# A DeltaNet encoder layer on one core: the first 16 tokens' products widened to 128 rows, and the inner products of a scan step moved into the next step

## Chip, core and metric

The kernel runs on one core of a Trainium2 chip. The metric is the device time of one execution in microseconds (us). The engines are TensorE (PE, with its weight loads as PEld), VectorE (DVE), ScalarE (ACT), GpSimd (POOL) and SyncE (SP), which issues most transfers.

## What is computed

One layer of an encoder over 16 learned tokens and 1024 tokens of input, D_MODEL 1024, 8 heads of 128. The part that the change touches is the gated delta rule, run forward and backward over the tokens in chunks, and summed:

```python
def step(S, inp):
    qk_c, qd_c, kd_c, u_c, w_c, gl_c = inp
    v_new = u_c - jnp.einsum("bhcd,bhde->bhce", w_c, S)
    o_c = (jnp.einsum("bhcd,bhde->bhce", qd_c, S)
           + jnp.einsum("bhij,bhje->bhie", qk_c, v_new))
    S = S * gl_c[..., None, None] + jnp.einsum("bhcd,bhce->bhde", kd_c, v_new)
    return S, o_c
...
o_fwd = chunk_gated_delta_rule(qp, kp, vp, gp[:, :, 0], bp[:, :, 0])
o_bwd = flip(chunk_gated_delta_rule(flip(qp), flip(kp), flip(vp), flip(gp[:, :, 1]), flip(bp[:, :, 1])))
o = (o_fwd + o_bwd)[:, META_PAD:]
```

Around it stand the input projection (q, k, v, z and gates), a short convolution as a second branch, the merge of both, an output projection, and a feed-forward block.

## The kernel before

**First part: dense products with scans in between.** The input projection runs as "units" of 128 output columns. A unit is `dense_steps` (L328): for each piece of tokens (320 to 512 columns) 24 products in a high/low split (hh, hl, lh). Between these dense products stand the steps of four streams, one head at a time in each: `g_decay`, `g_norm` (L537: transposes and squares of k and q, products k k and k q), `g_inv` (L640: inverse of the triangular blocks, L727 to L768) and `g_scan` (L772: the scan). A generator `yield`s the planned time at which it may go on; `run_streams` resumes it once PE's planned clock `T["pe"]` has got there. `pe(ns)` advances that clock, and `on(engine, ns)` books an operation of another engine, never earlier than PE's planned clock:

```python
T[e] = max(T[e], ready, T["pe"]) + ns
return T[e] + TOPE
```

So the planned times alone decide how many dense products stand between two groups of a stream. The program's order on each engine is written out by this plan; no engine leaves it when it runs. A head starts its stages when the heads ahead of it have freed what they hold. When the units are used up, the streams go on without dense work.

**The first 16 tokens ("meta").** They are a chunk of their own, number 8 in the head's tiles. `g_norm` transposes their k (L98 from L562) and forms k k (L563); `g_inv` inverts a 16x16 block on POOL and loads it as `Pm` (L698); `g_scan` multiplies it with the scaled v (L803), scales the result on DVE (`w`, L806) and multiplies with `kn` (L808); the result is the first state S0 (L811).

**A step of the scan** (8 steps per head, both directions `d` in each, chunks c = i and 7-i):

- b1 = k S (L853), b2 = q S (L856), in one group; then on DVE r0 (L863);
- NP r0 (L869); then on ACT w (L876) and v2 (L881);
- kn w (L886), then the new S on DVE (L899);
- the inner products PQ v2 (L890), which later go into the output: `output` takes q S (L831 on ACT or L834 on DVE), and what is put into `pending` (L839 adds the inner product, L843 squares the sum on ACT) is done by `outputs()` in the following step, after r0.

b1 and b2 come from the three PSUM banks of `pss`. After the last step `norm` scales the head's output on DVE (L915 to L923), and it is transposed (L98) and stored (L940).

**Second part.** The list SECTION (L1623) orders what follows: four z units (`z4` to `z7`, `dense` at L134 to L136, 48 products each, whose low weights `wl` DVE makes at L179), and DVE's preparation of sums and low parts (b0 to b3, mA, mB; L179 and L1407), then pair products (`product`, L1441), which read these sums. Each engine's order is fixed here, too.

Of the kernel before, what the change touches and what calls it, by code (L numbers as in the profile page):

```python
# [8 lines left out]
F32 = mybir.dt.float32  # L9
# [7 lines left out]
P = 128  # L17
# [3 lines left out]
META = 16  # L21
# [27 lines left out]
def encoder_layer(ctx: ExitStack, tc: tile.TileContext, x, meta, norm1_w, w_in, w_ba,  # L49
                  dn_conv_w, A_log, dt_bias, dn_norm_w, sc_conv_w, w_bdn, w_bsc,  # L50
                  w_out, norm2_w, w_gu, w_down, final_w, out):
    nc = tc.nc
# [12 lines left out]
    def uid(s):  # L65
        cnt["n"] += 1
        return f"{s}_{cnt['n']}"
# [29 lines left out]
    def transpose(dst, src, n=P):  # L97
        nc.tensor.transpose(dst, src, ident[:n, :n])  # L98
# [159 lines left out]
    def pe(ns):  # L258
        T["pe"] += ns
        return T["pe"] + HOP  # L260
# [4 lines left out]
    def A(n):  # L265
        return on("act", 144 + 0.834 * n)
# [204 lines left out]
    def cs(c):  # L471
        return slice(META + c * P, META + (c + 1) * P)
# [64 lines left out]
    def g_norm(h, st_):  # L537
# [23 lines left out]
        pt = psd()  # L561
        transpose(pt[:META, :P], kT[:, 0:META])  # L562
        mm(pt[:META, P:P + META], kT[:, 0:META], kT[:, 0:META], start=True, stop=True)  # L563
        t = pe(120)
        nxt = tok(0)
        yield t
        nc.scalar.copy(kn[:META, 8], pt[:META, :P])
        A(P)
# [69 lines left out]
        enqueue("norm", norm_job(st_, ssk1, cc, ce, he, y, tmp, sk))  # L638

    def g_inv(h, st_):  # L640

        NP, Nm = st_["NP"], st_["Nm"]

        nd = dr.tile([4, NC, 2, 32, 32], F32, tag="nd", name=uid("nd"), bufs=2)
# [47 lines left out]
        for b in range(4):  # L694
            nc.sync.dma_start(NP[B(b), :, :, B(b)].rearrange("j c d i -> j (c d) i"), pd[b].rearrange("c d j i -> j (c d) i"))
        Pm = dn.tile([META, META], F32, tag="Pm", name=uid("Pm"), bufs=2)
        st_["Pm"] = Pm
        nc.sync.dma_start(Pm, pdm)  # L698

# [72 lines left out]
    def g_scan(h, st_):  # L772
# [12 lines left out]
        for grp in ((8, 0, 7), (1, 2, 3), (4, 5, 6)):  # L785
            pt = newbank()
            for i, c in enumerate(grp):
                if c == 8:
                    transpose(pt[:META, i], vT[:, 0:META])
                else:  # L790
                    transpose(pt[:, i], vT[:, cs(c)])
            yield pe(330)
            for i, c in enumerate(grp):
                p = META if c == 8 else P
                nc.scalar.activation(vS[:p, c], pt[:p, i], AF.Copy, scale=sk[:p, c:c + 1])
                A(P)
# [5 lines left out]
        bank = newbank()  # L802
        mm(bank[:META, 0], Pm, vS[:META, 8], start=True, stop=True)  # L803
        yield pe(215)
        w = dn.tile([P, P], F32, tag="w0", name=uid("w"))
        nc.vector.tensor_scalar(out=w[:META], in0=bank[:META, 0], scalar1=ce[:META, 8, 0:1], scalar2=None, op0=ALU.mult)  # L806
        yield V(P, 1)
        mm(bank[:, 1], kn[:META, 8], w[:META], start=True, stop=True)  # L808
        yield pe(215)
# [4 lines left out]
        seen = set()  # L814
        pending = []

# [5 lines left out]
        def output(b2, c, d, sums):  # L822
# [3 lines left out]
            if not sums:  # L826
                nc.scalar.copy(oacc[c], b2[:, 2 + d])
                A(P)
                return
# [17 lines left out]
        for i in range(NC):  # L847
# [4 lines left out]
            for d in act_:  # L852
                mm(b1[:, d], kT[:, cs(cd[d])], S[d], start=True, stop=True)  # L853
            t = pe(215 * len(act_))
            for d in act_:
                mm(b2[:, d], qT[:, cs(cd[d])], S[d], start=True, stop=True)  # L856
# [26 lines left out]
            if i < NC - 1:  # L883
# [3 lines left out]
                t = pe(430)  # L887
            yield tv
            for d in range(2):
                mm(b2[:, 2 + d], PQ[:, cd[d], d], v2[d], start=True, stop=True)  # L890
            t2 = pe(430)
            if i < NC - 1:
                yield t
                for d in range(2):
# [7 lines left out]
                    S[d] = Sn  # L902
            else:
                freed += 1
                yield t2
# [1238 lines left out]
```

## Time and profile before

| | |
|---|---|
| median of 3 runs | 1980.38 us (1978.99 to 1980.45) |
| the profiled execution | 1978.97 us |
| its span, first to last instruction | 1977.2 us |
| TensorE clock granted | 0.999 |
| last scan's first transposes of v (L98) | at 873.1 us |
| z units on PE | 932.4 to 976.0 us |

A row of the timeline reads: start, length, engine, line, operation, out<-in, shapes, and in brackets idle time of the engine before it and what ended it. For matmuls, "16*128 16x128" is the stationary tile (rows*columns) and the moving one (rows x columns); "x4" counts instructions, and a product of 32-bit floats is two. The length of a product reaches over the start of the next one, since products are pipelined. A row of a stretch of time reads: from:to, length, then for PE, PEld, DVE, ACT and POOL the busy time (and instructions), then PE's granted clock, the share of the DMA engines and GB/s. L12 is line 12 of the kernel before.

### The profile page before, as it was taken

To read this page: it belongs to the slowest core of one execution; us is meant where nothing else is said; L and a number is where in the kernel's file an instruction comes from. 1 tells how busy PE (TensorE), PEld (TensorE's weight loads), DVE (VectorE), ACT (ScalarE), POOL (GpSimd) and SP (SyncE) were. 2 spreads that over 40 slices of the span, in tenths; PEclk is the share of its full clock that TensorE was granted. 3 is DMA by queue.
4 is the path that set the end of the run, shared out by engine and by line. 5 is a ranking of instruction groups with operands and counts; after the bars stand their busy time and mean duration, and the time that the engine had idled before them with its cause. 6 is when DMAs were issued, how large, how long until landed. Compare 5 with 4: busy or idle time off the path is not lost.

```text
span 1977.2 us, 31834 instructions
## 1 busy us (share of the span) xinstructions
PE 1961.2 (99%) x11992; PEld 1715.3 (87%) x11992; DVE 1395.8 (71%) x3017; ACT 838.5 (42%) x1968; POOL 106.6 (5%) x407
## 2 busy tenths in 40 slices
PE   9999999999999999999999999999999999999998
PEld 8999999999999999888888888888888888888887
DVE  7888688888888888844954544469676766746575
ACT  6472354636464646344444221225333333334344
POOL 2011101010101010100000000000000000000000
PEclk9999999999999999999999999999999999999999
DMA  4122122222222212222236752123366654477654
GB/s 145 59 88 81 55 87 60 76 60 76 60 76 60 76 60 76 70 87 90 102 128 229 252 167 97 65 86 111 124 220 243 253 183 165 170 278 243 193 176 165
DMA packets 124703, 251.52 MB, mean 127 GB/s; under 512 B 44988, under 2 KB 46453, under 8 KB 122117
## 3 DMA queue, kind: packets, MB, share of 16 engines
q1 hardware_dynamic: 123957, 248.44, 37.7%
q8 instruction: 94, 1.54, 0.3%
q10 hardware_dynamic: 592, 1.05, 0.1%
q14 instruction: 60, 0.49, 0.1%
HBM read 181.20 MB, written 68.25 MB: 126 GB/s over the span
## 4 chain that ended last, share of the span: by engine, by line
PE 92%; DVE 3%; DMA 2%; ACT 1%; issue 1%; SPq 0%; POOL 0%; DVEq 0%; POOLq 0%; ACTq 0%
PE pm L328 30%; PE pd L1441 14%; PE pe L1441 7%; PE pm L1441 5%; PE pe L136 2%; PE pe L135 2%; PE pe L134 2%; PE pd L869 1%; PE pd L890 1%; PE pd L853 1%; PE pe L2051 1%; PE pe L2052 1%; PE pe L2050 1%; PE pd L856 1%; PE pe L590 1%; PE pd L886 1%
## 5 line engine op out<-in xcount | busy, mean ns | idle before, releaser
L328 PE MATMUL pm<-hTh,wh 128*128 128x320 f32 (+4 forms) x1248 | 428.3, 348 | 0.3 <-ACT hTh L1091 0.2
L328 PE MATMUL pm<-al,wh 128*128 128x320 f32 (+4 forms) x1248 | 427.4, 348 | 0.0
L328 PE MATMUL pm<-hTh,wl 128*128 128x320 f32 (+4 forms) x1248 | 425.8, 346 | 0.1
L328 PEld LDWEIGHTS pm<-hTh,wh 128*128 128x128 f32 x1248 | 233.8, 188 | 12.8 <-issue 2.1
L328 PEld LDWEIGHTS pm<-hTh,wl 128*128 128x128 f32 x1248 | 233.9, 188 | 10.6 <-issue 0.4
L328 PEld LDWEIGHTS pm<-al,wh 128*128 128x128 f32 x1248 | 233.9, 188 | 9.7
L102 DVE TENSOR_TENSOR al<-raw,ring_h 128x1024 fp32r<-128x1024 f32 x73 | 88.6, 1222 | 64.7 <-ACT ring_h L101 63.9
L101 ACT CAST ring_h<-raw 128x1024 fp32r<-128x1024 f32 x73 | 76.6, 1053 | 106.2 <-PE pe L2052 35.0
L350 DVE SCALAR_TENSOR_TENSOR kq<-ra,wc,kq 128x520 f32<-128x520 f32 x128 | 96.5, 754 | 4.7 <-ACT kq L380 3.4
L977 DVE TENSOR_TENSOR wl<-raw,wh 128x512 fp32r<-128x512 f32 x112 | 75.8, 687 | 31.4 <-ACT wh L980 30.9
L876 ACT ACTIVATE w<-pd,small 128x128 f32<-128x128 f32 x128 | 39.8, 363 | 125.2 <-PE pd L869 124.6
L483 DVE TENSOR_TENSOR tm<-fP,fN 128x135 f32<-128x135 f32 (+23 forms) x248 | 71.6, 289 | 5.4 <-POOL mP L682 1.0
L487 DVE TENSOR_TENSOR fP<-fP,tm 128x135 f32<-128x135 f32 (+23 forms) x248 | 71.4, 288 | 5.1
L980 ACT CAST wh<-raw 128x512 fp32r<-128x512 f32 x112 | 66.3, 621 | 3.7 <-issue 3.6
L101 ACT CAST wh<-raw 128x1024 fp32r<-128x1024 f32 x37 | 38.8, 1048 | 46.6 <-PE pm L135 14.8
L1989 ACT ACTIVATE b<-b 128x512 f32<-128x512 f32 x20 | 12.6, 631 | 104.5 <-DVE b L1407 104.5
L843 ACT ACTIVATE jk<-NP 128x128 f32<-128x128 f32 x64 | 19.9, 311 | 76.5 <-DVE NP L839 75.4
L1441 PE MATMUL pd<-b_hl,wh 128*128 128x512 f32 x168 | 51.9, 390 | 0.0
L899 DVE SCALAR_TENSOR_TENSOR S<-S,eGl,pd 128x128 f32<-128x128 f32 x104 | 31.5, 340 | 28.0 <-PE pd L886 27.9
L863 DVE SCALAR_TENSOR_TENSOR r<-pd,negEG,vS 128x128 f32<-128x128 f32 x120 | 36.7, 344 | 20.4 <-PE pd L853 20.2
L1407 DVE TENSOR_TENSOR b<-pd,b 128x512 f32<-128x512 f32 x21 | 14.5, 689 | 51.8 <-PE pd L1441 51.8
L102 DVE TENSOR_TENSOR wl<-raw,wh 128x1024 fp32r<-128x1024 f32 x37 | 45.1, 1218 | 7.4 <-ACT wh L101 7.3
(629 smaller groups left out, 4783.0 us busy)
## 6 DMA issues: line engine op xcount, KB each, us to landing
raw<-in_w_in_dram SPq DMA_DIRECT2D x72, 512.0 KB
raw<-in_w_gate_up_dram SPq DMA_DIRECT2D x44, 512.0 KB
sums<-in_w_down_dram SPq DMA_DIRECT2D x22, 512.0 KB
t_d<-sums SPq DMA_DIRECT2D x11, 1024.0 KB
raw<-s_d SPq DMA_DIRECT2D x44, 256.0 KB
raw<-t_d SPq DMA_DIRECT2D x44, 256.0 KB
act_d<-b SPq DMA_DIRECT2D x43, 256.0 KB
raw<-act_d SPq DMA_DIRECT2D x33, 256.0 KB
```

What stands on the lines that cost most here:

```text
L101: nc.scalar.copy(hi, src)
L102: nc.vector.tensor_tensor(out=lo, in0=src, in1=hi.bitcast(F32), op=ALU.subtract)
L134: mm(po[:m, :n], wh[:, k, :m], xhk[:, t0:t0 + n], start=(k == 0), stop=False)
L135: mm(po[:m, :n], wh[:, k, :m], xlk[:, t0:t0 + n], start=False, stop=False)
L328: mm(po[:, :n], ww[:, k], f(k)[:, t0:t0 + n], start=i == 0, stop=i == 3 * KT - 1)
L350: nc.vector.scalar_tensor_tensor(out=acc, in0=raw[:, h0 + t:h0 + t + hn], scalar=wc[:, t, col:col + 1], in1=acc, op0=ALU.mult, op1=ALU.add)
L483: nc.vector.tensor_tensor(out=tv, in0=fP[:, 0:r, j:j + 1].broadcast_to([P, r, n]), in1=fN[:, j:j + 1, j + 1:32].broadcast_to([P, r, n]), o ...
L487: nc.vector.tensor_tensor(out=fP[:, 0:r, j + 1:32], in0=fP[:, 0:r, j + 1:32], in1=tv, op=ALU.subtract)
L876: nc.scalar.activation(w[d], b2[:, 2 + d], AF.Copy, scale=ce[:, c, d:d + 1])
L977: nc.vector.tensor_tensor(out=u[1][1][:, k], in0=u[2][:, k], in1=u[1][0][:, k].bitcast(F32), op=ALU.subtract)
L980: nc.scalar.copy(u[1][0][:, k], u[2][:, k])
L1441: mm(po, x[:, k], at(y, k), start=i == 0 and not add_to, stop=i == 11, skip_group_check=add_to)
```

## The change

It has two parts. The products of the first 16 tokens are taken over 128 rows and columns: k and v are transposed for tokens 0 to 127, k k is formed for 128, and the three tiles around the inverse (`Pm` for even and odd heads, and `w`) are full 128x128 tiles, filled with zeros once, of which only the 16 rows are written. And the inner products of a step (but the last) are no longer issued after kn w; they go into a list `late` that the following step issues between b1 and b2. The copy of the inner product in steps without a q S goes into `pending`.

```diff
-        transpose(pt[:META, :P], kT[:, 0:META])
-        mm(pt[:META, P:P + META], kT[:, 0:META], kT[:, 0:META], start=True, stop=True)
+        transpose(pt[:, :P], kT[:, 0:P])
+        mm(pt[:, P:2 * P], kT[:, 0:P], kT[:, 0:P], start=True, stop=True)
...
-        nc.scalar.copy(kn[:META, 8], pt[:META, :P])
+        nc.scalar.copy(kn[:, 8], pt[:, :P])
...
-        Pm = dn.tile([META, META], F32, tag="Pm", name=uid("Pm"), bufs=2)
-        st_["Pm"] = Pm
-        nc.sync.dma_start(Pm, pdm)
+        if not wide:
+            wide.extend(dn.tile([P, P], F32, tag=f"wide{i}", name=uid("wide")) for i in range(3))
+            for t in wide:
+                nc.gpsimd.memset(t, 0.0)
+        Pm = st_["Pm"] = wide[h % 2]
+        nc.sync.dma_start(Pm[:META, :META], pdm)
...
-                if c == 8:
-                    transpose(pt[:META, i], vT[:, 0:META])
-                else:
-                    transpose(pt[:, i], vT[:, cs(c)])
+                transpose(pt[:, i], vT[:, 0:P] if c == 8 else vT[:, cs(c)])
...
-        mm(bank[:META, 0], Pm, vS[:META, 8], start=True, stop=True)
+        mm(bank[:, 0], Pm, vS[:, 8], start=True, stop=True)
         yield pe(215)
-        w = dn.tile([P, P], F32, tag="w0", name=uid("w"))
+        w = wide[2]
...
-        mm(bank[:, 1], kn[:META, 8], w[:META], start=True, stop=True)
+        mm(bank[:, 1], kn[:, 8], w, start=True, stop=True)
...
             if not sums:
-                nc.scalar.copy(oacc[c], b2[:, 2 + d])
-                A(P)
+                def copy():
+                    nc.scalar.copy(oacc[c], b2[:, 2 + d])
+                    A(P)
+                pending.append(copy)
                 return
...
             t = pe(215 * len(act_))
+            while late:
+                late.pop(0)()
             for d in act_:
                 mm(b2[:, d], qT[:, cs(cd[d])], S[d], start=True, stop=True)
...
-            yield tv
-            for d in range(2):
-                mm(b2[:, 2 + d], PQ[:, cd[d], d], v2[d], start=True, stop=True)
-            t2 = pe(430)
+            def inner(b2=b2, cd=cd, v2=v2):
+                for d in range(2):
+                    mm(b2[:, 2 + d], PQ[:, cd[d], d], v2[d], start=True, stop=True)
+                return pe(430)
             if i < NC - 1:
+                late.append(inner)
                 yield t
...
             else:
+                yield tv
+                t2 = inner()
                 freed += 1
                 yield t2
```

Line numbers of the changed kernel stand a little higher: its L801, L806, L858, L871, L888, L892 and L928 are L803, L808, L856, L869, L886, L890 and L923 of before, and from the end of `g_scan` on all are 5 higher.

PE's order in the first head's scan, before: kn w, one dense product, the inner products, and dense products again.

```order
L886 MATMUL pd_2679<-w_2693,kn_1259 128x128
L886 MATMUL pd_2679<-w_2695,kn_1259 128x128
L328 MATMUL pm_2712<-hTh,wl_2457 128x322
L890 MATMUL pd_2680<-v_347_2697,PQ_1268 128x128
L890 MATMUL pd_2680<-v_348_2699,PQ_1268 128x128
L328 MATMUL pm_2712<-hTh,wh_2456 128x322
```

In the changed kernel, at the start of the following step:

```order
L853 MATMUL pd_2738<-S_2726,kq_308 128x128
L853 MATMUL pd_2738<-S_2728,kq_308 128x128
L892 MATMUL pd_2684<-v_348_2701,PQ_1268 128x128
L892 MATMUL pd_2684<-v_349_2703,PQ_1268 128x128
L858 MATMUL pd_2739<-S_2726,kq_308 128x128
L858 MATMUL pd_2739<-S_2728,kq_308 128x128
```

The inner products now stand between k S and q S, ahead of everything that waits for r0.

PE's order in the last head's scan, before, from the first products of a step to NP r0:

```order
L853 MATMUL pd_11990<-S_11979,kq_9467 128x128
L853 MATMUL pd_11990<-S_11981,kq_9467 128x128
L856 MATMUL pd_11991<-S_11979,kq_9467 128x128
L856 MATMUL pd_11991<-S_11981,kq_9467 128x128
L328 MATMUL pm_12010<-hTh,wh_11826 128x512
L328 MATMUL pm_12010<-al_124,wh_11826 128x512
L328 MATMUL pm_12010<-hTh,wl_11827 128x512
L328 MATMUL pm_12010<-hTh,wh_11826 128x512
L869 MATMUL pd_11991<-r_2047_11996,NP_10427 128x128
L869 MATMUL pd_11991<-r_2048_11998,NP_10427 128x128
```

And in the changed kernel, from a step's first products to kn w:

```order
L853 MATMUL pd_11936<-S_11930,kq_9924 128x128
L853 MATMUL pd_11936<-S_11932,kq_9924 128x128
L892 MATMUL pd_11905<-v_1999_11924,PQ_10037 128x128
L892 MATMUL pd_11905<-v_2000_11926,PQ_10037 128x128
L858 MATMUL pd_11937<-S_11930,kq_9924 128x128
L858 MATMUL pd_11937<-S_11932,kq_9924 128x128
L871 MATMUL pd_11937<-r_2005_11944,NP_10697 128x128
L871 MATMUL pd_11937<-r_2006_11946,NP_10697 128x128
L136 MATMUL pm_12177<-hTh,wl_12144 128x512
L134 MATMUL pm_12177<-hTh,wh_12143 128x512
L135 MATMUL pm_12177<-al_126,wh_12143 128x512
L888 MATMUL pd_11936<-w_11952,kn_10451 128x128
```

The units of the first part are used up by now; what stands between the last scan's groups are products of z4 and z5 (pm_12177 is the second half of z4), three at a time. After the last inner product (L890, now L892) and ahead of the first pair product stood 36 products of L328 and 192 of the z units; now there are 121 of the z units: the rest of z5 (25 products), z6 and z7.

DVE's order at the end of the last scan, before; NP is the head's output, wl_12158 the low weights of z5, b_2067 the first of the sums:

```order
L923 TENSOR_SCALAR NP_10427<-NP_10427,small_10129 128x128 x7
L465 SCALAR_TENSOR_TENSOR rb_12067<-rb_12067,pm_12010 128x512
L923 TENSOR_SCALAR NP_10427<-NP_10427,small_10129 128x128
L179 TENSOR_TENSOR wl_12158<-raw_12139,wh_12157 128x1024
L465 SCALAR_TENSOR_TENSOR rb_12119<-rb_12119,pm_12069 128x512
L179 TENSOR_TENSOR b_2067_12135<-hTh 128x2048
L179 TENSOR_TENSOR b_2068_12136<-al_124 128x2048
```

In the changed kernel:

```order
L499 SCALAR_TENSOR_TENSOR small_10449<-small_10449 128x9
L928 TENSOR_SCALAR NP_10697<-NP_10697,small_10449 128x128 x8
L179 TENSOR_TENSOR b_2054_12125<-hTh 128x2048
L179 TENSOR_TENSOR b_2055_12126<-al_124 128x2048
L1510 SCALAR_TENSOR_TENSOR s_2070_12203<-s_2070_12203,pe_12150 128x512
L1412 TENSOR_TENSOR b_2054_12125<-b_2054_12125,b_2055_12126 128x2048
```

The low weights of z5 and the gate operations (L465) stand ahead of the last scan now; the first of the sums still comes right after the head's last scaling, and the low weights of z6 seven operations further on, as before.

More of the change, by code (lines that the diff above doesn't have):

```diff
@@ L638, in g_norm @@
         enqueue("norm", norm_job(st_, ssk1, cc, ce, he, y, tmp, sk))
+    wide = []
     def g_inv(h, st_):
@@ L787, in g_scan @@
             for i, c in enumerate(grp):
-                if c == 8:
-                    transpose(pt[:META, i], vT[:, 0:META])
-                else:
-                    transpose(pt[:, i], vT[:, cs(c)])
+                transpose(pt[:, i], vT[:, 0:P] if c == 8 else vT[:, cs(c)])
             yield pe(330)
             for i, c in enumerate(grp):
-                p = META if c == 8 else P
-                nc.scalar.activation(vS[:p, c], pt[:p, i], AF.Copy, scale=sk[:p, c:c + 1])
+                nc.scalar.activation(vS[:, c], pt[:, i], AF.Copy, scale=sk[:, c:c + 1])
                 A(P)
@@ L814, in g_scan @@
         seen = set()
-        pending = []
+        pending, late = [], []
         def outputs():
```

## Prediction

> **What bounds the kernel now.** I read the page first, for the engine that is full.
>
> ```profile
> span 1977.2 us, 31834 instructions
> PE 1961.2 (99%) x11992; PEld 1715.3 (87%) x11992; DVE 1395.8 (71%) x3017; ACT 838.5 (42%) x1968; POOL 106.6 (5%) x407
> ```
>
> TensorE (PE) has something in flight 99% of the span, so two things change the time: products that cost PE more or less, and places where PE's fixed order makes it wait. A busy PE is not proof of full speed, because the ends of products are modelled; so I price products by the distance from one start to the next, in PE's own timeline. For the one place where another engine follows closely behind PE, I then read the end of the last scan: PE's timeline, VectorE's (DVE's), and the busy time in two stretches.
>
> ```profile
> 922.89 0.61 PE L890 MATMUL pd<-v,PQ 128*128 128x128 f32 x4
> ...
> 975.97 0.39 PE L1441 MATMUL pd<-hTh,wh 128*128 128x512 f32 x1
> ...
> 981.41 0.61 PE L1441 MATMUL pd<-b,mB 128*128 128x512 f32 x2
> ```
> ```profile
> 923.54 0.61 DVE L834 SCALAR_TENSOR_TENSOR NP<-pd,eG,NP 128x128 f32<-128x128 f32 x2 [1.17 <-PE pd L890]
> ...
> 929.21 0.68 DVE L465 SCALAR_TENSOR_TENSOR rb<-rb,pm 128x512 f32<-128x512 f32 x1
> 929.81 0.28 DVE L923 TENSOR_SCALAR NP<-NP,small 128x128 f32<-128x128 f32 x1
> ...
> 939.64 2.29 DVE L179 TENSOR_TENSOR b<-hTh 128x2048 f32<-128x2048 f32 x1 [4.31 <-DMA z_d<-rb]
> ...
> 951.04 1.22 DVE L179 TENSOR_TENSOR wl<-raw,wh 128x1024 fp32r<-128x1024 f32 x1
> ...
> 977.55 2.35 DVE L179 TENSOR_TENSOR mB<-raw,mB 128x1024 fp32r<-128x1024 f32 x2
> ```
> ```profile
> 932.43:975.97 43.54, 43.54 (x193) 36.04 (x192) 37.94 (x31) 15.86 (x20) 0.00 (x0) 1.00 0.33 115
> 939.64:979.90 40.26, 40.26 (x180) 33.32 (x179) 40.05 (x32) 16.69 (x19) 0.00 (x0) 1.00 0.23 83
> ```
>
> The last inner product of the last scan starts at 922.89. DVE then finishes the head: 923.54 to 929.81+0.28 = 930.09, with one gate operation (L465, 0.68 long) in between. From 939.64 DVE prepares the sums for the pair products of L1441, without a gap (columns of the stretches: length, busy PE, weight loads, DVE: 40.05 of 40.26). PE meanwhile runs 192 products of the z units, 43.54/192 = 0.227 each, and reaches the first pair product at 975.97 and, at 981.41, the first that reads those sums (mB, whose first half is done at about 977.55+1.2 = 978.8). So DVE is ahead by 2.7 us only. That distance is the tightest thing I found, and the change moves it.
>
> **Part 1: products over 128 rows.** The two products of a head's first 16 tokens:
>
> ```profile
> 214.40 0.34 PE L328 MATMUL pm<-al,wh 128*128 128x384 f32 x1
> 214.67 0.39 PE L803 MATMUL pd<-vS,Pm 16*16 16x128 f32 x2
> ...
> 215.27 0.34 PE L328 MATMUL pm<-hTh,wh 128*128 128x384 f32 x1
> 215.44 0.34 PE L328 MATMUL pm<-al,wh 128*128 128x384 f32 x1
> ...
> 215.97 0.34 PE L328 MATMUL pm<-al,wh 128*128 128x384 f32 x1
> 216.23 0.48 PE L808 MATMUL pd<-w,kn 16*128 16x128 f32 x2
> ...
> 216.93 0.34 PE L328 MATMUL pm<-hTh,wh 128*128 128x384 f32 x1
> ```
>
> From 214.40 to 215.27 PE did two dense products and L803; a dense product of 384 columns takes 215.44-215.27 = 0.17, two of them 0.35, so L803 costs 0.87-0.35 = 0.52. L808 costs 0.96-0.35 = 0.61. What a product of full size costs is seen in the scan steps:
>
> ```profile
> 420.55 0.60 PE L886 MATMUL pd<-w,kn 128*128 128x128 f32 x4
> 420.91 0.40 PE L328 MATMUL pm<-hTh,wh 128*128 128x336 f32 x1
> 421.14 0.61 PE L890 MATMUL pd<-v,PQ 128*128 128x128 f32 x4
> ...
> 423.46 0.61 PE L853 MATMUL pd<-S,kq 128*128 128x128 f32 x4
> 423.90 0.61 PE L856 MATMUL pd<-S,kq 128*128 128x128 f32 x4
> 424.27 0.40 PE L328 MATMUL pm<-al,wh 128*128 128x336 f32 x1
> 424.51 0.31 PE L328 MATMUL pm<-hTh,wl 128*128 128x336 f32 x1
> 424.66 0.32 PE L328 MATMUL pm<-hTh,wh 128*128 128x336 f32 x1
> ```
>
> Eight instructions (four products) and one dense product take 424.51-423.46 = 1.05; less the dense one (424.66-424.51 = 0.15 to 0.16) that is 0.89, or 0.22 a product. So L803 gives back 0.30 and L808 0.39. The head's opening group becomes dearer in one place:
>
> ```profile
> 99.26 0.27 PE L98 MATMUL pe<-ident,kq 128*16 128x128 f32 x1
> 99.46 0.21 PE L563 MATMUL pe<-kq 128*16 128x16 f32 x2
> 99.61 0.66 PE L98 MATMUL pe<-ident,kq 128*128 128x128 f32 x4
> ...
> 100.28 0.33 PE L328 MATMUL pm<-hTh,wh 128*128 128x384 f32 x1
> ```
>
> It takes 1.02 with one dense product, 0.85 without. With full sizes it is one transposition (0.11, half a product), one product (0.22) and four transpositions (0.44): 0.77, so 0.07 is saved although L563 has eight times the columns. The wider transposition of vT I set at nothing. Per head 0.76, for eight heads 6.0 us; I keep 5 to 7.
>
> The weight loads speak on the other side:
>
> ```profile
> L563 PEld LDWEIGHTS pe<-kq x16: 92/94/97, 99.5 to 765.1; 128*16 128x16 f32 x16
> L590 PEld LDWEIGHTS pe<-kq x128: 186/188/191, 114.0 to 795.1; 128*128 128x128 f32 x128
> ```
>
> A load of 16 columns takes 94 ns, one of 128 columns 188. The scan products have loads of 128 columns too and still follow each other every 0.11, so loads lie beside products and I add nothing. The Trainium skill ("TensorE: Matmul & The Clock Gate", section LDWEIGHTS) says that a load's time goes by its columns, columns/1.2 ns, whatever the rows; by its figures six wider loads a head would, if uncovered, take back an estimated 8 x 6 x 0.093 = 4.5 us of the gain.
>
> The memsets of the three tiles run once, on POOL (5% busy), and only the first head's Pm transfer stands behind them in SP's queue, long before L803 needs it: nothing, or a microsecond of PE if that cover were gone. The copies on ACT go over more partitions with the same 128 columns: nothing.
>
> **Part 2: the inner products moved.** On PE alone this is worth nothing. L886 by itself costs 0.36 and makes the next dense product 421.14-420.91 = 0.23 instead of 0.16 long: 0.44 in all. L853 and L856 merged cost 0.89, twice that. A group fewer saves no time. What changes is when the planner lets the rest follow. A VectorE operation is booked no earlier than PE's planned clock, and the inner products now advance that clock by 430 ns between a step's first products and its r0. Each of seven steps gets longer in the plan, in each of eight heads, so the same dense products are used up by earlier scans. The order shows the end of it: in the last scan no L328 is left, z products stand between its groups, and after its last inner product stand 121 z products where before there were 36 L328 and 192 z products. So 36+71 = 107 dense products, 107 x 0.227 = 24.3 us of PE, have moved ahead of that inner product.
>
> Now the order on DVE decides. The first preparation operation (b<-hTh) still stands behind the last scaling of the last head. It no longer has the transfer of L465 ahead (the 4.31 us wait at 939.64), because those operations stand earlier now. So, counted from the start of the last inner product:
>
> - DVE finishes the head: 930.09-922.89-0.6 = 6.6.
> - From b<-hTh to the end of the low weights of z6: 951.04+1.22-939.64 = 12.6. PE cannot start z6 before. It has 25 z products (5.7), eight transpositions (0.9) and the inner products (0.4) until then: 7.0 of 19.2, so it stands still for 12.2.
> - Then z6, z7 (96 x 0.227 = 21.8) and the first two pair products (981.41-975.97 = 5.4).
>
> The first product on mB thus starts 6.6+12.6+21.8+5.4 = 46.4 after the last inner product, against 981.41-922.89 = 58.5 before: 12.1 less, where PE's work became 24.3 less.
>
> The last scan itself must go through with little dense work beside it. A step of before:
>
> ```profile
> 907.64 0.61 PE L853 MATMUL pd<-S,kq 128*128 128x128 f32 x4
> ...
> 913.09 0.61 PE L853 MATMUL pd<-S,kq 128*128 128x128 f32 x4
> ```
> ```profile
> 908.29 0.61 DVE L863 SCALAR_TENSOR_TENSOR r<-pd,negEG,vS 128x128 f32<-128x128 f32 x2 [0.76 <-PE pd L853]
> ```
> ```profile
> 909.13 0.31 ACT L843 ACTIVATE jk<-NP 128x128 f32<-128x128 f32 x1 [3.29 <-DVE NP L839]
> ...
> 910.09 0.63 ACT L876 ACTIVATE w<-pd,small 128x128 f32<-128x128 f32 x2
> ```
>
> r0 starts 0.65 after its products and takes 0.61: 1.26, and PE now has 3 x 0.44 = 1.33 of work before it needs it. That fits, and the two other hops of a step look alike. In the last four steps the two squares (jk) hold ACT for some 0.9 us from 1.5 us after the step's start, and w is wanted at about 2.0: w comes some 0.3 late. That makes 4 x 0.3 = 1.2, and I add 0.6 for the short inverse ahead of the scan: 1.8, with 0 (all covered) and 7 (every hop 0.3 late) as bounds.
>
> **The sum.** The last inner product: +24.3 of moved work, -6.0 saved, +1.8 waits = +20.1. From there to the first product on mB: -12.1. Net +8.0, and behind it PE has no idle time that could take it up. The profiled execution took 1978.97 us (span 1977.2 and 1.8 around it), 1.4 below the median of the runs, 1980.38. 1978.97+8.0 = 1987.0; on the median 1988.4. With 5 to 7 saved and 0 to 7 of waits: +5.2 to +14.2.
>
> **The rivals.** *Only the products count.* If PE's queue never waited, the change would be -6.0: 1974.4. It decides where z6's weights are ready before PE has worked off what stands ahead of z6. For it: PE was 99% busy and the saving is seen in every head. Against it: z6 needs weights that DVE makes 19.2 us after the last inner product, and PE has 7.0 of work. 7%.
>
> *A group fewer is worth something.* If the 0.08 by which a dense product behind a group is longer were the price of a switch, 56 groups fewer would save 4.5 more: 1988.4-4.5 = 1983.9. The merged pair at 0.89 speaks against it. 5%. The Trainium skill ("TensorEngine Tiling (Array Packing)", section Key Properties) puts the switch elsewhere: changing the tiling mode drains TensorE. With the 128 cycles that "TensorE: Matmul & The Clock Gate" (step 4, drain) gives for a drain, two switches at each of L803 and L808 are an estimated 1.7 us over eight heads, under the 5.5 of the rows.
>
> *The last scan crawls.* If a step there cannot go under the 913.09-907.64 = 5.45 of before (against 3.6 of PE's work, 3.9 with my waits), seven steps cost 11 more: 1999. For it: ACT and DVE hold other work; against it: the hops above. 10%.
>
> *They cancel*, within 4 us: 3%.
>
> **How the numbers follow.** Forecast 75% at 1988.4. About 0.2%, 4 us, is what a measurement of this kernel can tell from no change. Faster by more: 7%. Within: the second rival and the cancelling, 8%. Slower by more: 85%. The forecast's own range is 1985.6 to 1994.6; down to 1983 it takes in the second rival, and up to 1996 the lower part of the crawling scan.
>
> **What would show it.** Right: L801 and L806 at about 0.22 each; no L328 after the last vT; PE idle for some 12 us before z6's first product, released by DVE's wl; the first product on mB about 46 us behind the last inner one. Wrong: PE without idle time there (then -6), or idle inside each step of the last scan (then more than +14).

## The result, and the profile after

The changed kernel takes 1989.68 us in the median of 6 runs (1988.32 to 1990.71), beside 1979.57 for before (6 runs, 1978.99 to 1980.45). The ratio is 1.0051, with a 95% interval of 1.0040 to 1.0062: slower by 10.1 us. The prediction said 1988.4, which is 8.0 more than its median of before. The profiled execution took 1989.04, 10.07 more than that of before.

The page gives no hint by itself. TensorE (PE) is as full as it was, and its busy time has hardly moved (1961.2 us in before):

```profile
PE 1961.0 (99%) x11992; PEld 1718.6 (86%) x11992; DVE 1403.6 (71%) x3017; ACT 838.5 (42%) x1968; POOL 110.9 (6%) x410
```

First the products of the first 16 tokens, in PE's timeline:

```profile
214.59 0.34 PE L328 MATMUL pm<-al,wh 128*128 128x384 f32 x1
214.77 0.38 PE L801 MATMUL pd<-vS,wide 128*128 128x128 f32 x2
214.91 0.42 PE L328 MATMUL pm<-hTh,wl 128*128 128x384 f32 x1
215.16 0.34 PE L328 MATMUL pm<-hTh,wh 128*128 128x384 f32 x1
```

From 214.59 to 215.16 PE did two dense products (0.35) and L801: 0.22 for L801, where L803 had cost 0.52. Then the end of the last scan, PE and VectorE (DVE):

```profile
941.26 0.49 PE L892 MATMUL pd<-v,PQ 128*128 128x128 f32 x2
...
958.72 0.80 PE L134 MATMUL pm<-hTh,wh 128*128 128x512 f32 x1 [9.43 <-ACT wh L1497]
...
960.68 0.80 PE L136 MATMUL pm<-hTh,wl 128*128 128x512 f32 x1 [0.74 <-DVE wl L179]
...
963.83 0.63 PE L134 MATMUL pm<-hTh,wh 128*128 128x512 f32 x1
964.26 0.63 PE L135 MATMUL pm<-al,wh 128*128 128x512 f32 x1
...
989.49 2.88 PE L1446 MATMUL pd<-b,mB 128*128 128x512 f32 x12
```
```profile
946.32 1.66 DVE L928 TENSOR_SCALAR NP<-NP,small 128x128 f32<-128x128 f32 x8
...
959.41 1.22 DVE L179 TENSOR_TENSOR wl<-raw,wh 128x1024 fp32r<-128x1024 f32 x1
...
985.93 2.35 DVE L179 TENSOR_TENSOR mB<-raw,mB 128x1024 fp32r<-128x1024 f32 x2
```

The last inner product starts at 941.26 (before: 922.89), so 18.4 later. From there to the first product on mB PE takes 48.2 (before: 58.5), of which it stands still for 9.43 ahead of z6 and for 0.74 ahead of z6's third product. The first product on mB starts at 989.49 instead of 981.41: 8.1 later. DVE works without a gap from the last scaling to mB.

One thing is new: behind the idle time the products of z6 follow each other every 0.43 (963.83 to 964.26), nearly twice the 0.23 that they take from 965 on. The table of stretches gives the granted clock (the column with 1.00, 0.50, 1.00). It falls in the middle of the idle time and comes back at 964.76:

```profile
948.35:954.52 6.17, 0.94 (x5) 0.42 (x3) 6.17 (x4) 1.08 (x2) 0.00 (x0) 1.00 0.72 255
954.52:964.76 10.24, 5.30 (x12) 3.75 (x13) 10.14 (x11) 5.38 (x6) 0.00 (x0) 0.50 0.30 102
964.76:968.00 3.24, 3.24 (x16) 2.64 (x15) 3.24 (x3) 2.37 (x4) 0.00 (x0) 1.00 0.00 0
```

And the remaining 2.0 us (10.07 less 8.08) arise some 500 us later. There a product waits for an addition on DVE that had no wait in before; these are PE's rows of before and of the changed kernel:

```profile
1509.65 2.52 PE L1441 MATMUL pd<-b,w 128*128 128x512 f32 x10
```
```profile
1519.44 3.03 PE L1446 MATMUL pd<-b,w 128*128 128x512 f32 x12 [1.76 <-DVE b L1412]
```

### The profile page after: what moved, and what is told of

It is laid out like the page before. It is cut to its first block, busy times and chain, and to the rows that moved or that the text cites. A ratio compares the mean times of both kernels' runs of the same rounds, so it can differ in the third digit from the quotient of the medians.

```text
span 1987.3 us, 31900 instructions
## 1 busy us (share of the span) xinstructions
PE 1961.0 (99%) x11992; PEld 1718.6 (86%) x11992; DVE 1403.6 (71%) x3017; ACT 838.5 (42%) x1968; POOL 110.9 (6%) x410
## 4 chain that ended last, share of the span: by engine, by line
PE 93%; DVE 3%; DMA 2%; issue 1%; ACT 0%; SPq 0%; POOL 0%; DVEq 0%; ACTq 0%; POOLq 0%
PE pm L328 32%; PE pd L1446 13%; PE pe L1446 6%; PE pm L1446 4%; PE pd L892 1%; PE pe L135 1%; PE pe L134 1%; PE pe L136 1%; PE pd L871 1%; PE pd L853 1%; PE pd L858 1%; PE pe L590 1%; PE pd L888 1%; PE pe L2057 1%; PE pe L2055 1%; PE pe L2056 1%
## 5 line engine op out<-in xcount | busy, mean ns | idle before, releaser
L328 PE MATMUL pm<-hTh,wh 128*128 128x320 f32 (+4 forms) x1248 | 426.0, 347 | 0.4 <-ACT hTh L1096 0.2
L328 PE MATMUL pm<-al,wh 128*128 128x320 f32 (+4 forms) x1248 | 424.8, 346 | 0.0
L328 PE MATMUL pm<-hTh,wl 128*128 128x320 f32 (+4 forms) x1248 | 424.2, 345 | 0.0
L328 PEld LDWEIGHTS pm<-hTh,wh 128*128 128x128 f32 x1248 | 233.7, 188 | 11.8 <-ACT hTh L1096 0.9
L328 PEld LDWEIGHTS pm<-hTh,wl 128*128 128x128 f32 x1248 | 233.7, 188 | 10.8 <-POOL wl L1111 0.3
L328 PEld LDWEIGHTS pm<-al,wh 128*128 128x128 f32 x1248 | 233.8, 188 | 10.5
L1994 ACT ACTIVATE b<-b 128x512 f32<-128x512 f32 x20 | 12.6, 631 | 104.0 <-DVE b L1412 104.0
L379 ACT COPY ra<-pm 128x336 f32<-128x336 f32 (+2 forms) x72 | 32.1, 446 | 49.5 <-PE pm L328 49.0
```

The costliest lines, as they stand in the source:

```text
L328: mm(po[:, :n], ww[:, k], f(k)[:, t0:t0 + n], start=i == 0, stop=i == 3 * KT - 1)
L379: nc.scalar.copy(raw[:, 2 + t0:2 + t0 + n], po[:, :n])
```

## The experiments

Theory A was the prediction's: part 1 is worth what its rows say, and the loss is the work that now stands ahead of the last scan, because what follows hangs on DVE's chain from the last scaling. Its rivals: part 1 costs something itself, the moved products cost something where they stand, or the idle time of PE is the loss by itself.

**Part 1 alone, part 2 alone.** The first takes the changed kernel and puts the inner products back; the second takes the kernel before and has only the hunks on `late`, `inner` and `copy`.

> Part 1 alone (products of the first 16 tokens over 128 rows); the inner products stay where they were, so the planned order is that of before. Theory A (the loss comes only from the new order of the dense products around the last scans, and part 1 is worth what its rows say): L801 0.22 instead of L803's 0.52, L806 0.23 instead of 0.61, the opening group 0.77 instead of 0.84, eight heads: 6.0 us faster than before, about 1973.6. Rival B (wider weight loads eat most of it, 4.5 us): about 1.5 us faster, 1978. Rival C (part 1 itself brings the loss): slower than before.

> Part 2 alone (inner products moved into the next step), first 16 tokens as before. The order of the dense products is that of the changed kernel (121 z products behind the last inner product). Theory A: the changed kernel without its saving of 6.0, so 10.1+6.0 = 16 us slower than before, about 1995.7. If part 1 caused part of the loss: less than 10 us slower. If a group fewer per step were worth 4.5 us: about 11.5 us slower, 1991.

Part 1 alone: 1976.91 beside 1979.73, ratio 0.9984 (0.9975 to 0.9993), 2.8 us faster. On another chip:

> Part 1 alone beside the version with the later sums on the same chip: 1976.9.

1974.44 beside 1979.30, ratio 0.9975 (0.9966 to 0.9984), 4.9 faster. In the first profile the last inner product and the first product on mB are 5.4 earlier than in before:

```profile
917.48 0.39 PE L888 MATMUL pd<-v,PQ 128*128 128x128 f32 x2
```
```profile
976.01 0.39 PE L1439 MATMUL pd<-b,mB 128*128 128x512 f32 x1
```

922.89-917.48 = 5.4, and 981.41-976.01 = 5.4. So the saving is there, at nearly the size of the rows, and the wider loads do not eat it. This profile is of the fastest of the eleven runs, 1974.44, which is 4.5 less than the profiled execution of before. What the median lacks besides is in no trace; that it is lost behind, in waits that differ between executions (below), is not shown.

Part 2 alone: 1995.00 beside 1979.73, ratio 1.0073 (1.0061 to 1.0086), 15.3 us slower; 16 was expected, and 11.5 if a group fewer were worth something. It stands still for 9.44 ahead of z6, as the changed kernel does.

**Both parts, with the old plan.** The planner's clock is advanced where it was before; the products stay between k S and q S.

```diff
             def inner(b2=b2, cd=cd, v2=v2):
                 for d in range(2):
                     mm(b2[:, 2 + d], PQ[:, cd[d], d], v2[d], start=True, stop=True)
-                return pe(430)
+            yield tv
+            if i == NC - 1:
+                inner()
+            t2 = pe(430)
             if i < NC - 1:
                 late.append(inner)
...
             else:
-                yield tv
-                t2 = inner()
                 freed += 1
                 yield t2
```

> Both parts, but the planner is told of the inner products where they stood before (the clock advances behind kn w, not ahead of r0), so the units are taken in the order of before and 36 products of L328 and 190 of the z units stand behind the last inner product. The products themselves stand where the changed kernel has them, between k S and q S. Theory A (the planned order of the units is the whole loss): 6.0 us faster than before, 1973.6, and 16 faster than the changed kernel. Rival B (the inner products between k S and q S delay r0 and so each step): slower than part 1 alone by up to 56 x 0.3 = 17 us. Rival C (a group fewer is worth 0.08): 4.5 us faster than part 1 alone, 1969.

1980.93 beside 1979.73, ratio 1.0004 (0.9995 to 1.0013). So the plan accounts for some 9 us of the changed kernel's 10.1, and the idle time ahead of z6 is gone. But it is not 6 faster. Up to the last inner product this version is 4.5 us behind part 1 alone (921.94 against 917.48); more is lost behind the product on mB (last experiment). Its timeline shows places like this one, PE and then DVE:

```profile
336.24 0.75 PE L853 MATMUL pd<-S,kq 128*128 128x128 f32 x4 [0.33 <-DVE S L905]
337.11 0.68 PE L892 MATMUL pd<-v,PQ 128*128 128x128 f32 x4
```
```profile
336.36 0.61 DVE L834 SCALAR_TENSOR_TENSOR NP<-pd,eG,NP 128x128 f32<-128x128 f32 x2
```

k S waits for the new S. And the moved inner products start 0.87 behind k S instead of 0.45: they come 0.14 after the end of L834 (336.36+0.61 = 336.97), which DVE does right behind the new S. The inner products had been PE's work while DVE made S. Summed over all steps, it is 29.9 us from the first start of k S to the start of what follows it, and 27.1 in part 1 alone: 2.8 of the 4.5. The rest is not traced. To see whether their place does it, I put them ahead of k S:

```diff
+            while late:
+                late.pop(0)()
             for d in act_:
                 mm(b1[:, d], kT[:, cs(cd[d])], S[d], start=True, stop=True)
             t = pe(215 * len(act_))
-            while late:
-                late.pop(0)()
```

> The kernel with both parts and the old plan, with one difference: the moved inner products stand ahead of k S of the following step, not between k S and q S. They then lie again in the time in which VectorE makes the new S, as in before, and kn w, NP r0 and q S keep their distances. The version between k S and q S took 4.0 us more up to the last inner product than part 1 alone (278.1 against 274.1 beside the dense products). Theory D (the products were cover for the new S; without them k S waits for it in some steps): the 4.0 us come back, 274 beside the dense products, and the kernel takes what part 1 alone takes, 1976.9. Rival E (banks or the results held longer, whatever the place): 278 again, 1980.9.

1991.38 beside 1979.30, ratio 1.0058 (1.0046 to 1.0071): in the profiles the last inner product is 9.8 later than between k S and q S (931.76 against 921.94). Both expectations fail. The list of waits on PE names a wait that I had not seen (the wait in us, in how many places, the longest):

```profile
PE pd L892 <- DVE NP L834: 8.2, 15, 1.2
```

L834 takes q S out of the same PSUM tile that the inner product writes. In before the program wrote the inner product ahead of that operation; since the change it comes behind it, and has to wait for it (8.2 us in 15 places). Between k S and q S the four instructions of k S cover part of this wait, but not all of it at the place shown above. How the 4.5 us of the version before divide between the missing cover for S and this wait is not shown; this experiment cannot tell, because its own wait hides the answer.

**The plan's charge.** The moved products are not told to the planner at all.

```diff
-                return pe(430)
+                return pe(430 if i == NC - 1 else 0)
```

> Both parts; the moved inner products are not told to the planner at all (charge 0 instead of 430 ns; the last step's keeps its charge). The planned steps are then about as short as before (5.6 instead of 6.0 to 6.3), yet the units still come out in another order: three more units ahead of one head's last q/k/v unit, and only 96 z products behind the last inner product, 25 fewer than in the changed kernel. Theory A (the place of the last scan in the dense work decides, whatever the length of a planned step): 25 x 0.227 = 5.7 us slower than the changed kernel, about 1995.4. The step of my prediction that the charge of 430 ns ahead of r0 stretches every step and so moves the work: about as fast as with the old plan, 1974 to 1977.

2016.82 beside 1979.73, ratio 1.0184 (1.0170 to 1.0198): 37 us slower. My step on the 430 ns falls: without that charge the last scan starts even later (L801 at 936.75 instead of 908.22). Theory A named the side, but 5.7 us of the 27. In this kernel z4 and z5 are used up by the second step of the last scan, so nothing is left to put between its groups, and each hop, a wait for another engine's result, shows:

```profile
945.56 0.75 PE L853 MATMUL pd<-S,kq 128*128 128x128 f32 x4 [0.44 <-DVE S L902]
...
948.17 0.75 PE L888 MATMUL pd<-w,kn 128*128 128x128 f32 x4 [0.52 <-ACT w L878]
949.36 0.75 PE L853 MATMUL pd<-S,kq 128*128 128x128 f32 x4 [0.44 <-DVE S L902]
```

A step takes 949.36-945.56 = 3.80 with 2.2 of work in it, as much as a step of the changed kernel with 3.6 (3.79, below). So the scan without filling work is hardly shorter, 936.75 to 969.39 against 908.22 to 941.26, and the work that has moved ahead of it is paid for in full. That the hops set the length of a step is what comes true of the crawling scan; its 5.45 a step does not.

**Where the work moved.** The starts of a head's first product on `Pm` tell it: heads 5 and 6 in before, then in the changed kernel.

```profile
704.41 0.39 PE L803 MATMUL pd<-vS,Pm 16*16 16x128 f32 x2
...
801.88 0.39 PE L803 MATMUL pd<-vS,Pm 16*16 16x128 f32 x2
```
```profile
702.91 0.39 PE L801 MATMUL pd<-vS,wide 128*128 128x128 f32 x2
...
829.93 0.38 PE L801 MATMUL pd<-vS,wide 128*128 128x128 f32 x2
```

Up to head 5 nothing is later: 702.91 against 704.41. Head 6 is 28 us later at once. The units explain it: after head 5's q/k/v come three units of the other branch that must follow each other, then head 6's. A head's units are drawn only if the planner's clock has passed the end of the scan three heads earlier. By the program it is asked between units; in the changed kernel that scan's planned end falls just behind the question, so three more units are drawn first. One gate unit in that place lets it ask again earlier:

```diff
+    fill_units = fill_units[:21] + fill_units[27:28] + fill_units[21:27] + fill_units[28:]
```

> The changed kernel, with one gate unit (without followers) drawn ahead of the three units that came between head 5's and head 6's q/k/v units. Head 6's units are then taken one unit later than in before instead of three, and 147 z products stand behind the last inner product instead of 121. Theory A (each dense product moved ahead of the last scan costs its 0.227 us, because what follows hangs on VectorE's chain from the last scaling): 26 x 0.227 = 5.9 us faster than the changed kernel, about 1983.8. Rival (the idle time of PE before z6 is the loss, and it shrinks by 5.9 us at most with the same end): the same figure, but with the distance from the last inner product to the first product on mB at 48.2 instead of shorter; if that distance grows by 5.9, nothing is gained: 1989.7.

1983.98 beside 1979.14, ratio 1.0023 (1.0012 to 1.0033); 1983.8 was expected. Head 6 starts earlier than in the changed kernel, and the distance to mB is the same with 26 products more in it:

```profile
813.62 0.38 PE L801 MATMUL pd<-vS,wide 128*128 128x128 f32 x2
```
```profile
933.90 0.71 PE L892 MATMUL pd<-v,PQ 128*128 128x128 f32 x4
...
951.35 0.50 PE L134 MATMUL pm<-hTh,wh 128*128 128x512 f32 x1 [3.53 <-ACT wh L1498]
...
981.62 0.61 PE L1447 MATMUL pd<-b,mB 128*128 128x512 f32 x2
```

981.62-933.90 = 47.7 (changed kernel: 48.2), with 3.53 of idle time ahead of z6 instead of 9.43. Products put back behind the last inner product only fill idle time; what they bring is that the last scan comes earlier. That the median meets its figure is in part luck: in this profile, of the slowest of the seven runs (1986.60), the product on mB is 7.9 earlier than in the changed kernel and level with before (981.41), and the rest is lost behind it (last experiment). The order's 147 z products are still 81 fewer than before's 228 dense ones, some 18.4 us of PE, while head 6 slips by one unit only, 813.62-801.88 = 11.7. So the longer planned steps probably take a part too; no run separates the two.

**What bounds the stretch behind the last scan.** Two versions of the changed kernel, and the changed kernel again beside them:

```diff
-        z5h z4.0 z5l T1a z4.1 T1b z4.0t z4.0s T1c T2a z5.0 T1h z4.1t T2b z6h z4.1s u0h z6l u0l z5.1 z5.0t
+        z5h z4.0 z5l T1a z4.1 T1b z4.0t z4.0s z6h z6l T1c T2a z5.0 T1h z4.1t T2b z4.1s u0h u0l z5.1 z5.0t
```

> The changed kernel with z6's weights made earlier: the high part on ACT and the low part on VectorE stand behind the second operation of the sums (b<-al), five places earlier. PE's idle time before z6 then ends at about 955.5 instead of 960.7, 5 us earlier. Theory A (VectorE's chain from the last scaling to mB, 39.1 us without a gap, is the bound just behind PE): the first product on mB cannot come before about 987.2, so 2.3 us are gained at most, about 1987.5, and PE waits for mB instead. Rival (PE's idle time before z6 is the loss by itself): 5 us, 1984.7.

```diff
             a["po", i] = psz()
+            c0_ = C0 + META
+            for _ in range(40 if (h, i) == (6, 0) else 0):
+                mm(a["po", i], hx[0][:, 0, c0_:c0_ + P], hx[0][:, 0, c0_:c0_ + 512], start=True, stop=True)
             dense(a["po", i], a["w"], hx, C0 + META + 512 * i, 512)
```

> The changed kernel with 40 products without use (512 columns, 0.227 each, into the bank of z6's first half, which is then begun anew) in PE's idle time before z6, so that PE is busy until about 958.2. In the changed kernel the first nine or so products of z6 start 0.43 apart instead of 0.23 behind the idle time, and the granted clock in that stretch is 0.50. If idle time brings that clock down: z6's products start 0.23 apart, the first product on mB comes about 2.0 us earlier (487.5 instead of 489.5 within that thousand), and the kernel takes 1987.6. If the clock falls for another reason (the transfers, what VectorE does): no change, 1989.7.

(987.5 and 989.5 are meant.)

> The changed kernel itself beside the three variants on the same chip: 1989.7, with the first product on mB at 989.5 in its profile. What lies behind that product (gate, feed-forward) took 992.0 in before and 994.0 in the changed kernel's profile; if that difference is a transfer that lands late in some executions only, it differs here.

The changed kernel again: 1990.06 beside 1979.14, ratio 1.0056 (1.0043 to 1.0068), its first product on mB at 988.38, 47.8 behind its last inner product.

With z6's weights early: 1991.74, ratio 1.0056 (1.0042 to 1.0070): no gain. In its profile z6 starts at 952.87 instead of 958.72. Then PE waits elsewhere, and meets mB:

```profile
952.87 0.80 PE L134 MATMUL pm<-hTh,wh 128*128 128x512 f32 x1 [5.14 <-ACT wh L1497]
...
969.25 0.50 PE L136 MATMUL pm<-hTh,wl 128*128 128x512 f32 x1 [1.56 <-DVE wl L179]
...
987.08 3.02 PE L1446 MATMUL pd<-b,mB 128*128 128x512 f32 x12 [0.15 <-ACT s L1562]
```
```profile
952.85 1.23 DVE L179 TENSOR_TENSOR wl<-raw,wh 128x1024 fp32r<-128x1024 f32 x1 [1.30 <-ACT wh L1497]
...
985.75 2.35 DVE L179 TENSOR_TENSOR mB<-raw,mB 128x1024 fp32r<-128x1024 f32 x2
```

DVE's first half of mB ends at 985.75+1.22 = 986.97, and the product starts 0.11 behind it. (The profile puts its wait down to a copy on ACT that ends 0.06 after that half.) So 4.3 us less idle time ahead of z6 brought 0.8 up to mB (47.4 from the last inner product instead of 48.2), and nothing in the median. Part of that is the edit's own doing: DVE now waits 1.30 for ACT's high weights, and its chain gets 1.4 longer. In the changed kernel DVE has mB 2.3 us ahead of PE (985.93+1.22 = 987.15, product at 989.49), so no more than that was to be had. There, and in all its versions with DVE's old order, the scaling ends 6.7 us after the last inner product started, and mB's first half 39.2 after that, to within 0.02 us. That sum, 45.9, is the floor of this stretch; the changed kernel takes 48.2.

With 40 products in the idle time: 1986.34, ratio 1.0040 (1.0027 to 1.0053), an interval that overlaps that of the changed kernel. PE still waited for the low weights, and the products behind were again 0.43 apart (959.56 to 959.99):

```profile
957.10 0.50 PE L134 MATMUL pm<-hTh,wh 128*128 128x512 f32 x1 [0.37 <-ACT wh L1497]
...
959.05 0.72 PE L136 MATMUL pm<-hTh,wl 128*128 128x512 f32 x1 [1.22 <-DVE wl L179]
```

So I filled that wait as well, with 48 in place of 40:

> The version with products without use ahead of z6, with 48 of them instead of 40. With 40 the idle time left was 0.4 and 1.2 us, and after the second of these eight products of z6 still ran 0.43 apart. With 48, PE is busy until about 958.4 and waits for z6's low weights under 0.5 us. If idle time of about 1 us is what lowers the clock: all products of z6 0.23 apart, z7 begins 2.0 us earlier in relation to the last inner product, and the first product on mB about 1 us earlier, as VectorE's chain allows no more. If the clock falls for another reason: eight or more products at 0.43 again.

```profile
959.23 0.40 PE L134 MATMUL pm<-hTh,wh 128*128 128x512 f32 x1
959.47 0.40 PE L135 MATMUL pm<-al,wh 128*128 128x512 f32 x1
...
985.81 2.88 PE L1446 MATMUL pd<-b,mB 128*128 128x512 f32 x12
```

From there every product is 0.23 apart, and mB is met 985.81-939.46 = 46.4 behind the last inner product, 0.5 above the floor. So it was idle time that lowered the clock here, and pauses of 0.37 and 1.22 us were enough (longer ones elsewhere were not, see the last section). The time, 1988.51 beside 1979.30 (ratio 1.0049, 1.0036 to 1.0063), does not tell it from the changed kernel: at this place 2.3 us are to be had at most.

**What is lost far behind.** Part 1 alone, with the subtractions on the rows of w_down written later:

```diff
         add(u3, b1, u3)
+        while owed:
+            owed.pop(0)()
...
-            down_sums(j - 4, sg)
+            owed.append(down_sums(j - 4, sg))
```

(`down_sums` now issues its transfers and returns the subtractions and the store.)

> Part 1 alone, and the four subtractions on the rows of w_down (sums) are written behind the addition that frees a PSUM bank in the next pair (the transfers stay where they were); of these, the set at about 1505 us stands behind that addition on VectorE now, where it stood ahead of it. Part 1 alone had saved 5.4 us at the first product on mB, but only 2.8 in the median; its profile waits 0.7 us for that addition at 1505, and profiles of other variants 1.7 to 2.0, with a lower clock behind. Theory F (that wait, longer in some executions than in others, eats the rest): no wait there, 5 us faster than before, about 1974.5, and a spread under 3 us. If other waits take its place: 1976.9.

1973.59 beside 1979.30, ratio 0.9970 (0.9958 to 0.9981): the fastest version here, 5.7 us faster than before and faster than both kernels; its runs lie within 2.8 us. Part 1 alone on the same chip is 4.9 faster, so the two intervals overlap, and theory F is not shown, though the wait at that place is gone from its profile. What the profiles show is that this wait differs: none in before, 1.76 in the changed kernel, and each time DVE stands in front of a subtraction whose transfer of w_down has not landed (before, then the changed kernel):

```profile
1508.27 0.69 DVE L179 TENSOR_TENSOR sums<-sums 128x512 f32<-128x512 f32 x1 [3.42 <-DMA sums<-in_w_down_dram]
```
```profile
1518.10 0.69 DVE L179 TENSOR_TENSOR sums<-sums 128x512 f32<-128x512 f32 x1 [4.47 <-DMA sums<-in_w_down_dram]
```

Why it lands later in some executions stays open. The stretch behind mB is the same program in all these versions, and yet it differs by up to 7.5 us, one profiled execution each:

| | first product on mB | from there to the end of the span |
|---|---|---|
| before | 981.41 | 995.8 |
| part 1 alone | 976.01 | 996.7 |
| changed kernel | 989.49 | 997.8 |
| both parts, old plan | 980.01 | 1000.3 |
| z6's weights early | 987.08 | 1003.0 |
| one unit ahead | 981.62 | 1003.3 |

PE's waits in this stretch come to 0.3 us in before, 2.3 in the changed kernel and 4.5 in each of the last two. In the last three, the wait for that addition (1.97, 1.81 and 1.74) is also followed by products at half the clock (last section). Why these waits differ is not traced.

## Why the prediction was right, and where it was not

- **Part 1: right.** 0.22 for L801; last inner product and first product on mB 5.4 us earlier, where 6.0 (5 to 7) was said, and 2.8 and 4.9 faster in the medians. The wider loads cost nothing that shows. The Trainium skill's load time by columns ("TensorE: Matmul & The Clock Gate", section LDWEIGHTS) would have given back an estimated 4.5, if uncovered; part 1 alone agrees with the rows. (A load of 128 columns took 188 ns in the rows, more than the 107 of the Trainium skill's formula there; the 94 ns between a wide and a narrow load agree with it.)
- **A group fewer is worth nothing: borne out.** Part 2 alone was 15.3 slower; with the rival's 4.5 it would have been 11.5.
- **24.3 us moved ahead of the last inner product: the size was right, the reason only in part.** I wrote that each of seven steps gets longer in each of eight heads. The profile shows nothing later up to head 5, and 28 us at once at head 6: three units are drawn at a time. The charge of 430 ns is not what decides alone, since without it the last scan came later still. The step that failed is the one that takes the planned length of a step for the amount of work moved; reading the amount from the order, not from that rule, kept the sum right.
- **Waits in the last scan: the size was about right.** These rows of the changed kernel are the first products of two neighbouring steps, early and late in the last scan:

```profile
917.22 0.66 PE L853 MATMUL pd<-S,kq 128*128 128x128 f32 x4
...
921.01 0.28 PE L853 MATMUL pd<-S,kq 128*128 128x128 f32 x1
```
```profile
932.94 0.66 PE L853 MATMUL pd<-S,kq 128*128 128x128 f32 x4
933.35 0.47 PE L135 MATMUL pe<-al,wh 128*128 128x512 f32 x1
933.67 0.40 PE L136 MATMUL pe<-hTh,wl 128*128 128x512 f32 x1
...
937.36 0.28 PE L853 MATMUL pd<-S,kq 128*128 128x128 f32 x1
```

  A step takes 3.79 and 4.42. The early one holds the 3.6 of work that the prediction counted, with six z products; the late one holds eight, the two more behind k S, so about 4.0. That leaves 0.2 of waits in each of four steps, and 0.4 and 0.3 in the two late ones: 1.5, where I had set 1.8. My prices had w late in the last four steps by 0.3 and not at all in the early ones. The last inner product came at +18.4, not +20.1. A part of the difference stands in the lists of waits: ahead of the last scan PE of before waits 1.7 us at L590 and 1.6 at L739, PE of the changed kernel only 1.0 at a product of the same inverse, which is 2.3 less. I have not traced what takes those waits away.
- **DVE's order decides: right, and shown.** 6.7 to the end of the head (6.6 said), 12.6 to z6's low weights (12.6 said), 0.02 us of spread over the versions. PE's idle time was 10.2 instead of 12.2, chiefly because z6's first two products need only the high weights and fill 1.2 of it at half the clock. But the lower clock behind the idle time, which I had not thought of, took as much: 48.2 instead of 46.4 from the last inner product to mB. This miss (+1.8) and the one at the last inner product (-1.7) cancel, so +8.1 beside the predicted +8.0 is better than its parts.
- **"Behind it PE has no idle time that could take it up": right, but it can lose more.** 2.0 us came on top in the profile, in a stretch where PE works just behind DVE and DVE just behind a transfer; other versions lost up to 7.5 there.
- **Not seen at all:** the moved product now comes behind L831 and L834 in the program, and waits for them where they are late. In the changed kernel that is nearly covered; ahead of k S it cost 8.2 us.

## What to carry to other kernels

Where a planner deals out whole units of filler work, a small change of a planned time moves nothing or a whole batch: read the amount from the order, and look for the start that jumps. Before crediting filler work that moves, find the chain of the other engine that begins at the end of the scan; only what makes that chain start earlier is worth its full time. And an instruction that is postponed changes its place in the program against all readers of the tile that it writes.

## What the runs showed of the hardware

PE's clock fell after far shorter pauses than I had thought of, but not after every one of them. In the changed kernel it was 0.50 from 954.52, within the idle time of 9.43 us, to 964.76, and up to there the products of z6 were 0.43 apart. With 40 products in the idle time, pauses of 0.37 and 1.22 us within 2 us were followed by 0.43 again; with 48 the products were 0.23 apart at once. These are the slow stretches of the versions with z6's weights early and with the 40 products:

```profile
951.56:958.38 6.82, 5.48 (x12) 3.90 (x13) 5.50 (x3) 3.12 (x3) 0.00 (x0) 0.50 0.30 99
```
```profile
959.17:962.58 3.41, 3.41 (x9) 2.67 (x10) 3.38 (x6) 0.49 (x1) 0.00 (x0) 0.50 0.73 251
```

With the 10.24 of the changed kernel they are 3.41 long, and two and three times that. The length of a pause alone does not decide. The pause of 1.56 with z6's weights early (up to 969.25) left the clock at 1.00. And far behind, where twelve products take 3.03 after a pause of 1.76 in the changed kernel (1519.44, above), they take 4.43 after one of 1.74 in the version with one unit ahead:

```profile
966.50:970.00 3.50, 1.81 (x7) 0.97 (x6) 3.50 (x4) 0.90 (x2) 0.00 (x0) 1.00 0.32 129
```
```profile
1514.85 4.43 PE L1447 MATMUL pd<-b,w 128*128 128x512 f32 x12 [1.74 <-DVE b L1413]
```

What does decide is not shown here. The scan steps without filler (the version without the charge), with pauses of 0.4 to 0.5 twice in 3.8 us, ran at 1.00:

```profile
940.00:950.00 10.00, 8.32 (x58) 6.97 (x57) 3.57 (x13) 4.98 (x18) 0.00 (x0) 1.00 0.00 0
```

The Trainium skill ("TensorE: Matmul & The Clock Gate", Part 1) describes half the clock after an idle window of about 3.4 us. The half clock agrees with the 0.50 here, and so does 3.41 as the length of the shortest slow stretch; but pauses of 1.22 and of 1.74 us, short of that window, were enough in two of these runs.
